# An encoder layer on one core: the gathers of neighbourhood values on ScalarE's queue, and own buffers for the sine products

## The chip, the cores and the metric

The kernel runs on one NeuronCore of a Trainium2 chip. A core has five engines that run at the same time, each through its own queue in order: TensorE (PE) multiplies matrices, VectorE (DVE) and ScalarE (ACT) work on elements, GpSimd (POOL) does small element work and issues DMAs, SyncE (SP) issues DMAs. Sixteen DMA engines move data between the device's DRAM (HBM) and the on-chip memory SBUF, or from DRAM to DRAM. PE writes its results into PSUM, eight banks of 128 x 512 float32.

The metric is device time in microseconds (us) for one execution, the median of several runs. The profile comes from one further execution.

## What is computed

One layer of a bidirectional encoder on 1024 tokens of width 1024, in float32: a half-step SwiGLU feed-forward block, a token mixing block, a second half-step feed-forward block, each with normalisations around it. Cut to the token mixing, where the change lies:

```python
def _rotary(x, pos):
    ...
    cos, sin = jnp.cos(ang), jnp.sin(ang)
    x1, x2 = x[..., :half], x[..., half:]
    return jnp.concatenate([x1 * cos - x2 * sin, x1 * sin + x2 * cos], axis=-1)

def _token_mixing(u, w_in, ...):
    rq, rk, rv, rg, nq, nk, nv, g_ret, g_na = jnp.split(u @ w_in, points, axis=-1)
    q = _rotary(heads(rq, RET_QK_DIM), pos)
    k = _rotary(heads(rk, RET_QK_DIM), pos) * (RET_QK_DIM ** -0.5)
    y = _bidirectional_retention(q, k, heads(rv, RET_V_DIM), ...)
    ...
    y_ret = (jax.nn.silu(rg) * y) @ w_ret_out
    y_na = _neighborhood_attention(na_heads(nq), na_heads(nk), na_heads(nv), rel_bias) @ w_na_out
    merged = jax.nn.sigmoid(g_ret) * y_ret + jax.nn.sigmoid(g_na) * y_na
    return merged @ w_out
```

The neighbourhood attention sees the tokens as a grid of 16 rows by 64 columns. A block of 16 query columns looks at a window of 32 key columns, so the values nv are needed in four overlapping sets of columns (32 columns starting at 0, 8, 24 and 32).

## The kernel before

**Arithmetic.** Every float32 operand of a matrix product is split into a high part, a copy cast on ACT (L62), and a low part, the difference, on DVE (L63). A product of two split operands is three matmuls (L94 to L96). Weights come in by SP as blocks of 128 x 1024 (`wraw`, four buffers, L73) and are split into pieces `wh` and `wl`, eight buffers each.

**Winograd pairs.** Most of the projection u @ W runs in `Pairs`: a job takes two weight blocks g and u (512 KB each) and forms seven products of 128 x 512 in place of eight, named by the left operand: a11, s2, a12, s3, s1, a22, s4, in this order on PE, 12 matmuls each. The weight side needs sums of blocks: t1 (L550 or L574), t2 (L551 or L575), t3 (L587), t4 (L593 or L603). The four results c11, c12, c21, c22 are built on DVE out of the PSUM banks: L572 copies the first product on ACT, then come L578, L583, L590, L598, L600, L605 and L608. L608 is the last of a job; its instruction is kept as `mx.end`. Within a job, once its own last pieces are split, `prepare(i + 1)` loads the next job's two blocks and forms and splits what its first products need; the low part of the last piece prepared is kept as `mx.ahead`.

**The stage of the change.** The loop at L1434 runs 14 jobs. Jobs 0 to 3 make the attention's queries and keys. After job 3 the second half of nv is projected (`vproj`, L1463) and stored by POOL to DRAM as d["nv"]; then, before the change, SP issues four copies, DRAM to DRAM, that gather nv into the four column sets d["nvg"] (L1466, 1 MB each). Jobs 4, 6, 8 and 10 are the rotary ones (one head of queries and keys each), 5, 7, 9 and 11 the silu gates, 12 and 13 two sigmoid gates. The attention stage, which reads nvg (L966), begins after job 13.

**A rotary result.** For each of a rotary job's four parts, `done` (L1441) first carries out the swaps that are pending, then calls `rotate`: DVE multiplies the part by the sine table into a buffer t (L1110) and by the cosine table in place (L1111); POOL stores the cosine product to rq or rk. The swap, carried out when the next part is done, adds the two halves of t crosswise to what was stored, by two accumulating DMAs on POOL (L1115, L1116). Before the change, the parts and the buffers t take turns in one set of six buffers of 128 x 512 (`half()`, tag "ev").

**What sets the order.** A planner orders each engine's queue ahead of the run, by its own model of time; data dependencies and the reuse of buffers become semaphores. `c.after(e, names)` (L76) adds an edge that bears on the order alone (class NoSync).

Of the kernel before, what the change touches and what calls it, by code (L numbers as in the profile page):

```python
# [11 lines left out]
F32 = mybir.dt.float32  # L12
# [7 lines left out]
P = 128  # L20
# [8 lines left out]
NHP = 4  # L29
# [6 lines left out]
KEY_OFF = (0, 8, 24, 32)  # L36
# [1070 lines left out]
def rotate(c, t, x, cos, sin, dst, behind):  # L1107

    tt = c.nc.vector.tensor_tensor
    c.after(tt(t, x, sin, ALU.mult).ins, behind)  # L1110
    tt(x, x, cos, ALU.mult)  # L1111
    c.store(dst, x)

    def swap():
        c.nc.gpsimd.dma_start(dst[0:64], t[64:128], accum_op=ALU.add)  # L1115
        c.nc.gpsimd.dma_start(dst[64:128], t[0:64], accum_op=ALU.add)  # L1116
    return swap
# [159 lines left out]
def trunk_layer(ctx: ExitStack, tc, x, xt, g1a, w1i, w1o, g1b, gma, wmt, wnv, wrv, logits, dtab, rope, bias,  # L1277
                wro, wno, wmo, gmb, g2a, w2i, w2o, g2b, out):
    nc = tc.nc
# [5 lines left out]
    c = Core(tc, const, wpool, psum, dram)  # L1285
# [3 lines left out]
    def dt(name, shape):  # L1289
        return dram.tile(shape, F32, name=name)  # L1290
# [3 lines left out]
    d = {  # L1294
        "a21": dt("a21", [P, 4, 512]),
        "nq": dt("nq", [NHP, P, S]), "nk": dt("nk", [NHP, P, S]), "nv": dt("nv", [16, 64, 512]), "nvg": dt("nvg", [4, 4, P, 512]),
        "no": dt("no", [NHP, P, S]), "rq": dt("rq", [RH, P, S]), "rk": dt("rk", [RH, P, S]),
        "rv": dt("rv", [TT, P, D]), "rg": dt("rg", [8, P, S]), "ry": dt("ry", [8, P, S]),
        "dec": dt("dec", [P, 536]), "far": dt("far", [3, 2, P, 512]), "far1": dt("far1", [3, 2, P, 512]), "far2": dt("far2", [3, 2, P, 512]), "sr": dt("sr", [8, P, S]), "sn": dt("sn", [8, P, S]), "z": dt("z", [8, P, S]), "m": dt("m", [8, 2, P, S]),
    }  # L1300
# [6 lines left out]
    def pool(stack, name, side="left"):  # L1307
        return stack.enter_context(tc.tile_pool(name=name, bufs=1, side=side, reuse_waits="tile"))
# [52 lines left out]
    def vproj(src, groups, done):  # L1361

        w = []
        for toks in groups:
            banks = {t: c.bank() for t in toks}
            for k in range(KT):
                if k == len(w):
                    w += ahead.pop(k // 2) if k // 2 in ahead else c.load_w(src[k // 2])
                    if k > 3 and qk:
                        c.after(c.fetch, qk)  # L1370
                        qk.clear()
                for t in toks:
                    tt = slice((t % 4) * P, (t % 4 + 1) * P)
                    c.mm3(banks[t], [q[:, k % 4, tt] for q in xh(t // 4, k // 4)], w[k], k == 0, k == KT - 1)
                    yield
            for t in toks:
                done(t, banks[t])
# [27 lines left out]
    mx = Pairs(c, wx, [(wmt[j[0]], wmt[j[1]]) for j in jobs], 3, joined=False)  # L1405
# [15 lines left out]
    with tc.tile_pool(name="pa", bufs=1, reuse_waits="tile") as pa:  # L1421
        evpool[:] = [pa]
        fill.drain()
        swaps = []

        def half():
            return pa.tile([P, 512], F32, tag="ev", name="ev", bufs=6)

        tabs = [[pa.tile([P, 512], F32, tag="tab", name="tab", bufs=4) for _ in range(2)] for _ in range(2)]
        for h in range(2):  # L1430
            for j in range(2):
                nc.sync.dma_start(tabs[h][j], rope[:, j, h * 512:(h + 1) * 512])

        for i, (_, _, f, g, fn) in enumerate(jobs):  # L1434
            parts = {}

            def part(j):
                parts[j] = half()
                return parts[j]

            def done(j):  # L1441
                h = j % 2
                dst = (f, g)[j // 2][:, h * 512:(h + 1) * 512]
                while swaps:
                    swaps.pop()()
                if fn == "rotary":
                    swaps.append(rotate(c, half(), parts[j], *tabs[h], dst, [] if j == 0 else [mx.ahead]))
                    return
                if fn is not None:
                    nc.scalar.activation(parts[j], parts[j], fn)  # L1450
                c.store(dst, parts[j])
            mx.run(i, part, done, i not in (NHP - 1, len(jobs) - 1))
            if i == 2:
                x1pool = pool(x1_stack, "x1b", "right")
                a21[:] = [x1pool.tile([P, 4, 512], F32R, name=f"a21{q}") for q in "hl"]
                for k in range(2):
                    raw = c.raw(d["a21"][:, 2 * k:2 * k + 2].rearrange("p k t -> p (k t)"))
                    c.split(*[q[:, 2 * k:2 * k + 2].rearrange("p k t -> p (k t)") for q in a21], raw)
            if i == NHP - 1:
                dec = pa.tile([P, 536], F32, name="dec")  # L1460
                Decays(dec).make(c, pa, logits, dtab)
                c.store(d["dec"], dec)
                for _ in vproj(wnv, ((4, 5, 6, 7),), done_nv):  # L1463
                    pass
                for cb in range(4):
                    nc.sync.dma_start(d["nvg"][cb].rearrange("t (r c) d -> (t r) c d", r=4),  # L1466
                                      d["nv"][:, KEY_OFF[cb]:KEY_OFF[cb] + 32, :])
    left.close()

    m_stack, o_stack = ExitStack(), ExitStack()  # L1470
# [55 lines left out]
    tabs = mix.tile([P, 536], F32, name="dec")  # L1526
# [181 lines left out]
```

## Time and profile before

| | |
|---|---|
| median of 3 runs | 2209.81 us (2209.61 to 2209.9) |
| the profiled execution | 2210.64 us |
| its span, first to last instruction | 2208.9 us |
| granted TensorE clock | 0.999 of full speed |
| share of ACT and POOL busy | 43% and 27% |
| data moved | 444.63 MB, mean 201 GB/s |

How to read the rows below. A row of the table by windows has the stretch and its length in us, then the busy time of PE, of PE's weight loads (PEld), of DVE, ACT and POOL with the number of instructions, then the granted clock, the mean busy share of the DMA engines, and GB/s. A row of the timeline has start and duration in us, engine, line of the code, operation, what is written and read by the program's names, shape and count; in brackets stands the engine's idle time just before and what ended it. A row of one line of the code has its count, the least, median and greatest duration in ns, and the first and last start in us. SPq is SP's queue, on which issuing a DMA takes time; "DMA to landing" is from issue until the data are there. One matmul of 512 columns shows 0.39 us, but the next starts 0.227 us later, since they overlap.

### The profile page before, as it was taken

How to read it: one execution, taken by the hardware profiler on the slowest of the kernel's cores; microseconds unless marked ns; L12 is line 12 of the kernel's file. 1: busy time of each engine (PE TensorE's matmuls, PEld its weight loads, DVE VectorE, ACT ScalarE, POOL GpSimd, SP SyncE). 2: the span in 40 equal slices, each digit the busy share in tenths (PEclk: the TensorE clock that was granted, in tenths of full speed). 3: DMA queues.
4: the chain of work that ended last, by engine and by line, in shares of the span. 5: the costliest groups of instructions: out<-in, count | busy, mean ns of one | idle time of the engine just before them, and what ended most of it. 6: DMA issues, size and time to landing. Idle time of an engine off the chain costs nothing.

```text
span 2208.9 us, 29722 instructions
## 1 busy us (share of the span) xinstructions
PE 2186.8 (99%) x10232; PEld 1824.4 (83%) x10232; DVE 1574.1 (71%) x2767; ACT 959.9 (43%) x1970; POOL 588.7 (27%) x766
## 2 busy tenths in 40 slices
PE   8999999999999999999999999999999999999998
PEld 7878888888888888888888888888888888888887
DVE  7898887655569757777766677643999787867444
ACT  7444434322345322367775565322544343433232
POOL 2122212169421122311001222101112121216942
PEclk9999999999999999999999999999999999999999
DMA  7354544597745555575543466785446343549865
GB/s 267 129 194 173 200 167 169 220 374 284 246 174 188 197 170 145 146 237 180 184 168 128 145 210 222 272 303 185 156 153 226 130 170 133 181 170 373 276 224 185
DMA packets 151206, 444.63 MB, mean 201 GB/s; under 512 B 19472, under 2 KB 46224, under 8 KB 148944
## 3 DMA queue, kind: packets, MB, share of 16 engines
q1 hardware_dynamic: 107584, 302.97, 40.7%
q0 software_dynamic: 43472, 139.77, 17.6%
q8 instruction: 81, 1.33, 0.2%
q14 instruction: 69, 0.57, 0.1%
HBM read 294.54 MB, written 152.32 MB: 202 GB/s over the span
## 4 chain that ended last, share of the span: by engine, by line
PE 90%; DVE 4%; issue 3%; ACT 1%; DMA 1%; POOL 1%; POOLq 0%; SPq 0%; DVEq 0%; ACTq 0%
PE ps L94 28%; PE ps L95 28%; PE ps L96 28%; PE pt L95 1%; PE pt L94 1%; PE pt L96 1%; PE pt L1002 1%; PE ps L983 1%; DMA g0s<-gth 1%; PE pt L133 0%; DVE wl L63 0%; PE pt L1216 0%; POOL rstd L104 0%; DMA gt<-in_dram 0%; POOL g0a L69 0%
## 5 line engine op out<-in xcount | busy, mean ns | idle before, releaser
L63 DVE TENSOR_TENSOR wl<-wraw,wh 128x512 fp32r<-128x512 f32 x440 | 292.4, 686 | 54.1 <-ACT wh L62 53.3
L62 ACT CAST wh<-wraw 128x512 fp32r<-128x512 f32 x444 | 255.2, 618 | 135.2 <-PE ps L95 57.4
L94 PE MATMUL ps<-wh,g 128*128 128x512 f32 x548 | 214.1, 391 | 0.4 <-DVE tmp L231 0.4
L95 PE MATMUL ps<-wl,g 128*128 128x512 f32 x548 | 213.6, 390 | 0.0
L96 PE MATMUL ps<-wh,g 128*128 128x512 f32 x548 | 213.3, 389 | 0.0
L63 DVE TENSOR_TENSOR wl<-w,wh 128x512 fp32r<-128x512 f32 x77 | 78.8, 1044 | 83.9 <-ACT wh L62 83.7
L63 DVE TENSOR_TENSOR wl<-x,wh 128x512 fp32r<-128x512 f32 x77 | 79.9, 1054 | 76.1 <-ACT wh L62 74.6
L62 ACT CAST wh<-t 128x512 fp32r<-128x512 f32 x58 | 36.1, 622 | 212.2 <-DVE t L575 130.4
L94 PEld LDWEIGHTS ps<-wh,g 128*128 128x128 f32 x548 | 102.9, 188 | 22.0 <-DVE tmp L231 0.7
L95 PEld LDWEIGHTS ps<-wl,g 128*128 128x128 f32 x548 | 102.9, 188 | 21.4 <-DVE wl L63 0.7
L96 PEld LDWEIGHTS ps<-wh,g 128*128 128x128 f32 x548 | 102.9, 188 | 21.3
L94 PE MATMUL ps<-a11h,wh 128*128 128x512 f32 x276 | 108.7, 395 | 1.5 <-ACT a11h L62 1.5
L94 PE MATMUL ps<-a22h,wh 128*128 128x512 f32 x280 | 109.7, 392 | 0.0
L95 PE MATMUL ps<-a11l,wh 128*128 128x512 f32 x276 | 107.9, 391 | 1.3 <-DVE a11l L63 1.3
L95 PE MATMUL ps<-a22l,wh 128*128 128x512 f32 x280 | 109.1, 390 | 0.0
L96 PE MATMUL ps<-a22h,wl 128*128 128x512 f32 x280 | 109.0, 389 | 0.0
L96 PE MATMUL ps<-a11h,wl 128*128 128x512 f32 x276 | 107.7, 390 | 0.9 <-DVE wl L63 0.9
L94 PE MATMUL ps<-a12h,wh 128*128 128x512 f32 x276 | 108.2, 393 | 0.0
L95 PE MATMUL ps<-a12l,wh 128*128 128x512 f32 x276 | 107.5, 390 | 0.0
L96 PE MATMUL ps<-a12h,wl 128*128 128x512 f32 x276 | 107.5, 389 | 0.0
L62 ACT CAST wh<-w 128x512 fp32r<-128x512 f32 x77 | 46.6, 620 | 110.8 <-PE pt L96 54.5
L69 POOL DMA_DIRECT2D g1a<-gth x33 | 17.9, 543 | 285.1 <-ACT gth L672 284.3
(444 smaller groups left out, 6305.5 us busy)
## 6 DMA issues: line engine op xcount, KB each, us to landing
wraw<-in_dram SPq DMA_DIRECT2D x190, 512.0 KB, 4.4
g<-g0s SPq DMA_DIRECT2D x44, 512.0 KB, 4.2
g<-g1s SPq DMA_DIRECT2D x44, 512.0 KB, 4.5
g<-g0a SPq DMA_DIRECT2D x33, 512.0 KB, 4.7
g<-g1a SPq DMA_DIRECT2D x33, 512.0 KB, 4.7
g0s<-gth POOLq DMA_DIRECT2D x44, 256.0 KB, 4.0
g0s<-cmb POOLq DMA_DIRECT2D x44, 256.0 KB, 3.9
g1s<-gth POOLq DMA_DIRECT2D x44, 256.0 KB, 3.9
```

What stands on the lines that cost most here:

```text
L62: self.done = [nc.scalar.copy(h, src).ins, (eng or nc.vector).tensor_tensor(l, src, hf, ALU.subtract).ins]
L63: (eng or nc.vector).tensor_tensor(l, src, hf, ALU.subtract).ins]
L69: self.nc.gpsimd.dma_start(dst, src)
L94: mm(ps, a[0], b[0], start=start, stop=False, skip_group_check=again)
L95: mm(ps, a[0], b[1], start=False, stop=False, skip_group_check=again)
L96: self.tail = mm(ps, a[1], b[0], start=False, stop=stop, skip_group_check=again).ins.name
L983: nc.tensor.matmul(bv, q[:, rg * P:(rg + 1) * P], k, start=n == 0, stop=n == 1)
L1002: nc.tensor.transpose(pt[:, j * P:(j + 1) * P], s[:, i % 2, (i // 2) * P:(i // 2 + 1) * P], c.ident)
```

## The change

The buffers t of the rotary jobs come from a set of four of their own (tag "evt"); the parts keep the six "ev" buffers to themselves. The four gathers of nv are written one job later in the program, after job 4 (`i == NHP`) in place of job 3, on ACT's queue in place of SP's, with an ordering edge behind the last DVE instruction of job 4 (`mx.end`).

```diff
                 if fn == "rotary":
-                    swaps.append(rotate(c, half(), parts[j], *tabs[h], dst, [] if j == 0 else [mx.ahead]))
+                    swaps.append(rotate(c, pa.tile([P, 512], F32, tag="evt", name="evt", bufs=4), parts[j], *tabs[h], dst, [] if j == 0 else [mx.ahead]))
                     return
...
                 for _ in vproj(wnv, ((4, 5, 6, 7),), done_nv):
                     pass
+            if i == NHP:
                 for cb in range(4):
-                    nc.sync.dma_start(d["nvg"][cb].rearrange("t (r c) d -> (t r) c d", r=4),
-                                      d["nv"][:, KEY_OFF[cb]:KEY_OFF[cb] + 32, :])
+                    c.after(nc.scalar.dma_start(d["nvg"][cb].rearrange("t (r c) d -> (t r) c d", r=4),
+                                                d["nv"][:, KEY_OFF[cb]:KEY_OFF[cb] + 32, :]).ins, [mx.end.name])
```

## The prediction

> **What bounds the kernel now.** I began with the page's busy times, then cut the span into stages with the table of busy time by windows, then asked what TensorE (PE) waited for.
>
> ```profile
> PE 2186.8 (99%) x10232; PEld 1824.4 (83%) x10232; DVE 1574.1 (71%) x2767; ACT 959.9 (43%) x1970; POOL 588.7 (27%) x766
> 0.00:100.00 100.00, 92.38 (x409) 75.61 (x410) 80.85 (x130) 58.07 (x109) 13.27 (x21) 1.00 0.51 184
> 100.00:780.00 680.00, 677.35 (x3012) 558.76 (x3011) 509.52 (x807) 267.45 (x502) 222.70 (x275) 1.00 0.60 215
> 780.00:840.00 60.00, 60.00 (x266) 49.68 (x265) 34.03 (x54) 17.40 (x30) 15.11 (x23) 1.00 0.66 197
> 840.00:860.00 20.00, 19.07 (x84) 15.27 (x83) 16.02 (x27) 5.08 (x9) 7.77 (x11) 1.00 0.41 82
> 860.00:960.00 100.00, 100.00 (x442) 82.82 (x442) 75.13 (x121) 37.91 (x64) 27.64 (x41) 1.00 0.60 162
> 960.00:1000.00 40.00, 39.32 (x198) 32.61 (x197) 27.05 (x69) 25.12 (x59) 6.13 (x8) 1.00 0.80 259
> 1000.00:1400.00 400.00, 398.19 (x2272) 347.46 (x2271) 283.61 (x734) 255.17 (x650) 72.00 (x109) 1.00 0.55 178
> 1400.00:1600.00 200.00, 199.20 (x909) 164.69 (x908) 118.72 (x192) 72.20 (x150) 23.25 (x40) 1.00 0.65 230
> ```
>
> PE is busy for 2186.8 of 2208.9 us, so all its idle time is 22.1 us, and 10.3 us of it lie before 780, where the change does not reach (7.6 in the first 100 us, 2.65 in the next 680). The change lies between about 787 us, where job 4 begins, and 940. There PE loses time in one stage only, 840 to 860. The rows of PE and of VectorE (DVE) at that place say why:
>
> ```profile
> 787.51 0.39 PE L94 MATMUL ps<-a11h,wh 128*128 128x512 f32 x1
> 806.55 0.39 PE L94 MATMUL ps<-a11h,wh 128*128 128x512 f32 x1
> 825.59 0.39 PE L94 MATMUL ps<-a11h,wh 128*128 128x512 f32 x1
> 844.63 0.39 PE L94 MATMUL ps<-a11h,wh 128*128 128x512 f32 x1
> 846.18 0.50 PE L96 MATMUL ps<-a11h,wl 128*128 128x512 f32 x1 [0.93 <-DVE wl L63]
> 865.05 0.39 PE L94 MATMUL ps<-a11h,wh 128*128 128x512 f32 x1
> 844.83 0.69 DVE L608 TENSOR_TENSOR ev<-ps,ev 128x512 f32<-128x512 f32 x1 [2.03 <-PE ps L96]
> 845.44 0.68 DVE L63 TENSOR_TENSOR wl<-wraw,wh 128x512 fp32r<-128x512 f32 x1
> 846.15 0.69 DVE L550 TENSOR_TENSOR wraw<-wraw 128x512 f32<-128x512 f32 x1
> ```
>
> The five a11h,wh rows are the first matmuls of jobs 4 to 8. Jobs 4, 5 and 6 take 19.04 us each (806.55 - 787.51, and so on): seven products of 2.72 us. Job 7 takes 865.05 - 844.63 = 20.42, so the stall and the matmuls just behind it cost **1.38 us**. PE waited for the low part (L63) of job 7's first weight piece, and on DVE that stood in the queue behind L608 of job 6, which needs job 6's last product. Job 7's whole preparation (L550 and what follows) came behind it too. So in this stage the wait that ends last is one of DVE's order, not of DVE's speed.
>
> **The change, part by part.** First, the gathers (L1466): four copies of 1 MB, DRAM to DRAM, leave SyncE's (SP's) queue for ScalarE's (ACT's), behind L608 of job 4.
>
> ```profile
> L1466 SPq DMA_DIRECT2D nvg<-nv x4: 557/718/1382, 793.3 to 796.2; - x4
> L1466 SPq EVENT_SEMAPHORE  x2: 28/3231/6434, 786.8 to 793.3; - x2
> DMA to landing us min/median/max: 7.0/10.4/13.1
> 793.33 3.51 SPq L1466 DMA_DIRECT2D nvg<-nv  x4
> 816.77 14.24 SPq L73 DMA_DIRECT2D wraw<-in_dram  x4
> 814.68 0.59 ACT L572 COPY ev<-ps 128x512 f32<-128x512 f32 x1 [11.79 <-PE ps L95]
> 816.05 1.90 DVE L63 TENSOR_TENSOR wl<-wraw,wh 128x512 fp32r<-128x512 f32 x3
> ```
>
> SP loses a wait of 6.43 us and 3.51 us of issue. Behind them stands the weight load (L73) at 816.77, which waits for the first of the three L63 at 816.05 (it ends at 816.7), 20 us after the gathers were issued. So SP's relief is worth **0** by itself. On ACT, no DMA is issued in this trace. The bounds are 0 and SP's longest, 4 x 1.382 = 5.5 us; I take SP's 3.51, the same four copies. The wait on the stores of nv is over by 793.3, before job 4's L608, so it costs nothing. The edge that is added (the helper at L76) only orders; it sets no semaphore. PE ends job 4 at 806.55, so ACT can issue from about 807.2 to 810.7, at the far bound to 812.7. Behind it stands job 5's copy L572, whose product is done at 806.55 + 2.72 = 809.3 and which ran at 814.68 before; PE wants that bank back only six products later, at 806.55 + 6 x 2.72 = 822.9. Cost **0**, from both bounds. If that cover were gone, the price would be the same 3.5 us.
>
> Second, the sine products (L1110) no longer take turns in the six ev buffers.
>
> ```profile
> 798.31 0.54 POOL L69 DMA_DIRECT2D rq<-ev  x1 [9.18 <-DVE ev L1111]
> 809.81 0.89 POOL L1115 DMA_DIRECT2D rq<-ev  x1 [10.96 <-DMA rq<-ev]
> 809.61 0.69 DVE L1110 TENSOR_TENSOR ev<-ev,tab 128x512 f32<-128x512 f32 x1 [3.97 <-DMA rq<-ev]
> 814.07 0.69 DVE L1110 TENSOR_TENSOR ev<-ev,tab 128x512 f32<-128x512 f32 x1 [1.36 <-DMA rq<-ev]
> 820.74 0.69 DVE L590 TENSOR_TENSOR ev<-ps,ev 128x512 f32<-128x512 f32 x1 [1.41 <-DMA rk<-ev]
> 793.30:805.60 12.30, 12.30 (x56) 10.20 (x55) 9.51 (x15) 2.19 (x4) 0.54 (x1) 1.00 0.99 347
> 826.19 1.14 POOL L1116 DMA_DIRECT2D rk<-ev  x1
> 834.67 0.69 DVE L1110 TENSOR_TENSOR ev<-ev,tab 128x512 f32<-128x512 f32 x1
> ```
>
> The first store of rq, issued at 798.31 while the gathers held the DMA engines (share 0.99 from 793.3 to 805.6), took about 11 us, and DVE stood still for a buffer: 3.97 + 1.36 + 1.41 = 6.74 us in three waits. All three should go: the store no longer meets the gathers, and the product has a buffer of its own. What that moves is the weight load, which waits for L63: two of the waits stand ahead of 816.05, so the load for job 6 can go out up to 5.33 us earlier, at about 811.4. PE did not wait in these 6.74 us (60.00 of 60.00 busy), so by itself this is also worth **0**. It pays only through job 6 and job 7: with DVE, loads and pieces of job 6 earlier, job 7's preparation can stand ahead of L608 as it does in every other job, and the 1.38 us go. Bounds: 0 and 1.38. The new buffers bring a wait of their own: four hold one rotary job's products, so job 6's first (834.67) waits until the last accumulation of job 4 (issued at 826.19) has read its buffer. 8.5 us lie between, and what would queue behind it on DVE is L1111 and L590, beside a busy PE: 0. Of the whole part I take 1.38: the two late things ahead of this place, gathers and buffer waits, are the very ones the change removes.
>
> Third, memory: four buffers of 512 x 4 bytes, 8 KB a partition, in the pool's top.
>
> ```profile
> 936.57 1.13 POOL L1116 DMA_DIRECT2D rk<-ev  x1
> L940 SPq DMA_DIRECT2D qraw<-nq x16: 450/589/605, 957.5 to 1084.7; - x16
> ```
>
> Their last reader is issued at 936.57; even at the gathers' 13.1 us it lands by 949.7. The attention stage, which reuses this memory, loads from 957.5. Cost 0.
>
> **Sum**: 0 + 0 - 1.38 + 0 = -1.4 us. The profiled execution took 2210.64 (span 2208.9), 0.83 above the median of the runs, 2209.81. So 2209.3 for a profiled execution, **2208.4** as median. About 0.2%, or 4.4 us, is what a measurement of this kernel can tell from no change. All idle time of PE from 780 to 1600 is 0.93 + 0.68 + 1.81 + 0.80 = 4.2 us, so there is not even room for a gain of that size in the stages that follow.
>
> **Rivals.** *It is hidden altogether.* DVE's order is fixed ahead of the run by a planner, and the profile does not say why it put job 7's preparation late. If it stays so, every saved wait lies beside a busy PE, and the time is 2209.8. For it: PE shows no idle time at either removed wait. Against: the two causes of lateness are gone. The Trainium skill, "DMA: Bandwidth & Descriptors", section "Issuing engines are not separate DMA queues", says that issuing from several engines saves only the issuer's time, small beside the transfer; by that rule the first part gives nothing, and the trace agrees (SP had nothing ready to issue before 816.77).
>
> *The gathers now collide with the weight loads, and the kernel is slower.* They were in flight from 793 to about 809; they move to about 807 to 823, and there lie the loads for job 6 and the rotary stores and accumulations:
>
> ```profile
> 816.80:822.00 5.20, 5.20 (x25) 4.30 (x24) 3.70 (x6) 2.17 (x3) 2.30 (x4) 1.00 1.00 208
> 821.35 0.68 DVE L550 TENSOR_TENSOR wraw<-wraw 128x512 f32<-128x512 f32 x1
> L62 ACT CAST wh<-wraw 128x512 fp32r<-128x512 f32 x444 | 255.2, 618 | 135.2 <-PE ps L95 57.4
> wraw<-in_dram SPq DMA_DIRECT2D x190, 512.0 KB, 4.4
> ```
>
> The DMA share there is already 1.00. Job 6's load landed in time for L550 at 821.35, and PE needs the piece's low part at 825.59 + 0.23 = 825.8; a cast (0.62) and L63 (0.69) lie between, so landing after 824.5 stalls PE. Issued at 816.77 and taking 13.1 us like the slowest gather, it would land at 829.9: a stall of 5.4 us, 2215.2. Issued at 811.4, the same 13.1 us land just at 824.5 and cost nothing. So it decides only where the load does not move ahead, or takes even longer. The Trainium skill, same page, section "Queues, rings and completion order", has each DMA engine take turns between the queues; by that rule a load on SP's queue would take about twice its usual 4.4 us beside ACT's (an estimate) and land by 820, with no stall. No run here has two such queues at once.
>
> *The planner's order shifts further on.* The stages from 960 to 1600 lose 0.68 + 1.81 + 0.80 = 3.3 us in short waits; another order could win part of them or add as much: 2206 to 2212.
>
> **Chances.** The stall goes and nothing else moves (2208.4, say 2207.9 to 2208.9): 0.47. Hidden (2209.8): 0.26. Collision (2210 to 2215.2): 0.15, of which 0.04 by over 4.4 us. Order elsewhere: 0.12, of which 0.02 beyond 4.4 us faster and 0.01 slower. So faster 0.02, within 0.2% 0.93, slower 0.05. The range reaches over the first two cases, the milder half of the collision and most of the last: 2207.0 to 2211.2.
>
> **What would show it.** Right: no wait of PE between 840 and 860, and job 7 taking 19.04 us; no wait of L1110 for a DMA of rq; the gathers' issues on ACT near 807, with L572 behind them not late for PE; job 6's load near 811. Wrong: PE waiting for a wl or wh at the start of job 6 near 825.6 (collision), job 7 still at 20.4 (hidden), or other waits after 960 (order).

## The result and the profile after

| | before | after |
|---|---|---|
| median | 2210.09 us (2208.85 to 2211.95, 22 runs) | 2213.07 us (2211.84 to 2215.88, 22 runs) |
| the profiled execution | 2210.64 | 2211.95 |
| its span | 2208.9 | 2210.2 |

After over before is 1.0014, with a 95% interval of 1.0008 to 1.002: about 3.0 us slower. That lies within the 0.2% forecast as "same", but above the range, and on the other side of the 1.4 us gain that was predicted.

First the table by windows of after; its columns are those of the prediction's table (length, PE, PEld, DVE, ACT, POOL, granted clock, DMA share, GB/s).

```profile
710.00:730.00 20.00, 16.20 (x69) 12.44 (x68) 14.38 (x47) 3.55 (x8) 2.16 (x4) 1.00 0.34 119
780.00:840.00 60.00, 60.00 (x267) 49.69 (x266) 34.71 (x55) 17.72 (x30) 14.05 (x21) 1.00 0.65 193
840.00:860.00 20.00, 20.00 (x90) 16.58 (x89) 15.80 (x26) 4.96 (x9) 6.93 (x9) 1.00 0.65 144
860.00:960.00 100.00, 100.00 (x443) 82.84 (x442) 74.83 (x121) 38.13 (x64) 29.45 (x43) 1.00 0.56 152
```

From 780 to 960 PE never stands still: the stall of 840 to 860 is gone, as forecast. But from 710 to 730, some 60 us ahead of every line that the diff touches, PE is busy for 16.20 of 20 us. The prediction had no row of that stage. Here is its row of the kernel before, with PE's wait there, the first DVE instruction of the retention's decays, and the two loads on SP that will matter:

```profile
710.00:730.00 20.00, 19.23 (x85) 15.58 (x85) 15.70 (x44) 4.37 (x10) 2.71 (x5) 1.00 0.32 112
716.65 0.50 PE L94 MATMUL ps<-s1h,wh 128*128 128x512 f32 x1 [0.78 <-DVE ev L586]
705.92 0.17 DVE L1074 TENSOR_SCALAR dect<-decx 128x8 f32<-128x8 f32 x1
692.76 2.24 SPq L1432 DMA_DIRECT2D tab<-in_dram  x4
695.04 0.47 SPq L1071 DMA_DIRECT2D decx<-in_dram  x1
```

And the timeline of after, PE, then DVE, then SP:

```profile
717.04 0.50 PE L94 MATMUL ps<-s1h,wh 128*128 128x512 f32 x1 [2.44 <-DVE ev L586]
720.24 0.50 PE L94 MATMUL ps<-a22h,wh 128*128 128x512 f32 x1 [0.18 <-DVE ev L590]
724.47 0.50 PE L94 MATMUL ps<-s4h,wh 128*128 128x512 f32 x1 [1.18 <-ACT ev L572]
705.27 0.69 DVE L583 TENSOR_TENSOR ev<-ps,ev 128x512 f32<-128x512 f32 x1 [0.26 <-ACT ev L572]
714.68 0.17 DVE L1074 TENSOR_SCALAR dect<-decx 128x8 f32<-128x8 f32 x1 [8.72 <-DMA decx<-in_dram]
716.30 0.69 DVE L586 TENSOR_TENSOR ev<-ps,ev 128x512 f32<-128x512 f32 x1
704.62 1.88 SPq L1432 DMA_DIRECT2D tab<-in_dram  x4
706.54 1.00 SPq L1071 DMA_DIRECT2D decx<-in_dram  x1
```

Read from the bottom. The load of `decx` (L1071), 128 x 8 numbers from which the decays of the retention are made, goes out at 706.54 where it went out at 695.04, and so do the rotary tables ahead of it (704.62 in place of 692.76). The decays' first DVE instruction that reads it (L1074) stands at the head of DVE's queue and waits 8.72 us for it; before, it ran at 705.92 without a wait. Behind it in that queue is L586 of job 0, the instruction that empties a PSUM bank that PE wants: PE stands for 2.44 us. Two waits of 0.18 and 1.18 us follow while DVE and ACT catch up; before, one wait of 0.78 was there.

The first matmuls of jobs 4, 7 and 8 make the account:

```profile
789.88 0.39 PE L94 MATMUL ps<-a11h,wh 128*128 128x512 f32 x1
847.00 0.39 PE L94 MATMUL ps<-a11h,wh 128*128 128x512 f32 x1
866.04 0.39 PE L94 MATMUL ps<-a11h,wh 128*128 128x512 f32 x1
```

Job 4 begins at 789.88 against 787.51 before, 2.37 us late. Job 7 takes 866.04 - 847.00 = 19.04 us against 20.42, so 1.38 are won back, and job 8 begins 0.99 late. The two spans differ by 1.3. The medians differ by 3.0; the profiled execution of after was one of its fastest (2211.95, where the lowest of 22 runs is 2211.84), and the runs of one kernel differ by up to 3.1 us before and 4.0 after, so a single pair need not show the difference of the medians. The last section comes back to the 1.7 us that this pair does not show.

### The profile page after: what moved, and what is told of

It reads as the page before. It is cut to its first block, busy times and chain, and to the rows that moved or that the text cites. A ratio compares the mean times of both kernels' runs of the same rounds, so it can differ in the third digit from the quotient of the medians.

```text
span 2210.2 us, 29703 instructions
## 1 busy us (share of the span) xinstructions
PE 2186.6 (99%) x10232; PEld 1824.4 (83%) x10232; DVE 1573.5 (71%) x2767; ACT 959.8 (43%) x1970; POOL 586.5 (27%) x766
## 4 chain that ended last, share of the span: by engine, by line
PE 86%; DVE 5%; issue 4%; ACT 2%; DMA 2%; POOL 1%; SPq 0%; POOLq 0%; DVEq 0%; ACTq 0%
PE ps L94 27%; PE ps L95 27%; PE ps L96 27%; PE pt L94 1%; PE pt L96 1%; PE pt L95 1%; DVE wl L63 1%; PE pt L1002 0%; ACT s L988 0%; PE ps L983 0%; POOL rstd L104 0%; DMA no<-ot 0%; DMA decx<-in_dram 0%; PE pt L133 0%; DVE s L984 0%
## 5 line engine op out<-in xcount | busy, mean ns | idle before, releaser
L63 DVE TENSOR_TENSOR wl<-wraw,wh 128x512 fp32r<-128x512 f32 x440 | 292.8, 688 | 56.7 <-ACT wh L62 56.1
L63 DVE TENSOR_TENSOR wl<-w,wh 128x512 fp32r<-128x512 f32 x77 | 78.9, 1045 | 83.7 <-ACT wh L62 83.6
L63 DVE TENSOR_TENSOR wl<-x,wh 128x512 fp32r<-128x512 f32 x77 | 79.9, 1055 | 77.2 <-ACT wh L62 75.8
```

Source lines behind the costliest of these rows:

```text
L63: (eng or nc.vector).tensor_tensor(l, src, hf, ALU.subtract).ins]
```

## The experiments

**The theory.** The pool `pa` holds the buffers "ev", the rotary tables, the decays' small tiles and now "evt". It begins before job 0. In the program's memory map it takes bytes 128864 to 152768 of a partition before the change, and reaches 160960 after. At 153440 begin the tiles `cmb`, in which the sums of the Winograd operands are formed until about 704 (L299 at 701.71 and L300 at 702.92 write the last). The longer pool lies over them, so the plan opens it, as a whole, later; the loads of its tables come about 12 us later, and `decx` is late at the head of DVE's queue. **The rivals:** that the loss comes of the use of the four buffers or of the gathers' new place; or that any edit reshuffles the order.

The first two rows below are SP's weight loads beside these loads, before and after; the third is DVE's last read of `cmb`, after.

```profile
704.82 1.53 SPq L73 DMA_DIRECT2D wraw<-in_dram  x2
703.04 1.53 SPq L73 DMA_DIRECT2D wraw<-in_dram  x2
704.30 0.69 DVE L63 TENSOR_TENSOR s4l<-cmb,s4h 128x512 fp32r<-128x512 f32 x1
```

They say how the lateness reaches the run. Two weight loads that stood behind the loads of the pool before (704.82) stand ahead of them after (703.04), and the tables go out right behind, at 704.62. The last read of `cmb` lasts until 704.99, so the first of these loads did not wait for that memory in the run; the later opening acts through the place in SP's queue that the plan gives to the loads.

A first group of four takes the change apart. The ratios are to the kernel before, whose median was 2210.01 us in these comparisons. In `gathers_only` the sine products of the changed kernel go back into the six shared buffers:

```diff
-                    swaps.append(rotate(c, pa.tile([P, 512], F32, tag="evt", name="evt", bufs=4), parts[j], *tabs[h], dst, [] if j == 0 else [mx.ahead]))
+                    swaps.append(rotate(c, half(), parts[j], *tabs[h], dst, [] if j == 0 else [mx.ahead]))
```

> The four gathers on ACT's queue behind job 4, as in the change, but the sine products back in the six ev buffers. Theory (the new buffers do the harm, by making pool pa longer than 153440 bytes from the start of SBUF, onto the sums of the Winograd operands): no trace of it here. DVE does not wait for decx, PE is busy about 19.2 of the 20 us from 710 to 730 as before the change, and the time is 0 to 1.4 us below before. Rival (the gathers' new place makes the planner order the tables and the decays another way): PE busy 16 to 17 us from 710 to 730, and 1.5 to 4 us above before.

In `buffers_only` the same two lines are exchanged the other way in the kernel before, and the gathers stay where they were:

```diff
-                    swaps.append(rotate(c, half(), parts[j], *tabs[h], dst, [] if j == 0 else [mx.ahead]))
+                    swaps.append(rotate(c, pa.tile([P, 512], F32, tag="evt", name="evt", bufs=4), parts[j], *tabs[h], dst, [] if j == 0 else [mx.ahead]))
```

> Four buffers of their own for the sine products, the gathers back on SP's queue behind job 3. Theory (the buffers do the harm): DVE waits about 8.7 us for decx near 706, PE is busy about 16.2 us from 710 to 730, and the time is 2 to 4.5 us above before. Rival (the gathers' new place does it): 710 to 730 as before the change, time within 1.4 us of before. From 840 to 860 PE is busy 20.0 us if the buffers alone cure the wait at the start of job 7, 19.1 if the gathers are needed for it.

In `own_pool` the four buffers of the changed kernel lie at the same addresses, but in a pool that is opened before job 4:

```diff
...
+            if i == NHP:
+                spare.append(pool(t_stack, "evt"))
...
-                    swaps.append(rotate(c, pa.tile([P, 512], F32, tag="evt", name="evt", bufs=4), parts[j], *tabs[h], dst, [] if j == 0 else [mx.ahead]))
+                    swaps.append(rotate(c, spare[0].tile([P, 512], F32, tag="evt", name="evt", bufs=4), parts[j], *tabs[h], dst, [] if j == 0 else [mx.ahead]))
```

> The whole change, but the four buffers lie in a pool of their own at the same addresses, opened after job 3. Theory (what hurts is that pool pa as a whole waits for the memory that its longest end needs): tables and decays come as before the change, PE is busy 19.2 us from 710 to 730 and 20.0 from 840 to 860, and the time is 0.5 to 1.5 us below before. Rival (four more buffers in that memory hurt wherever they are declared, or the gathers do it): 16 to 17 us busy from 710 to 730, time 1.5 to 4 us above before.

In `decays_later` the pool is as long as in the change, and the decays' first DVE instructions (in `Decays.make`, L1074 and on) are ordered behind L608 of job 0, which is what `behind` holds:

```diff
-        nc.vector.tensor_scalar(a, x, -1.0, None, ALU.mult)
+        for op in (nc.vector.memset(s, 1.0 / 17.0), nc.vector.tensor_scalar(a, x, -1.0, None, ALU.mult),
+                  nc.vector.tensor_scalar(lg, x, 0.0, None, ALU.min)):
+            c.after(op.ins, behind)
...
-        nc.vector.memset(s, 1.0 / 17.0)
...
-        nc.vector.tensor_scalar(lg, x, 0.0, None, ALU.min)
...
-                Decays(dec).make(c, pa, logits, dtab)
+                Decays(dec).make(c, pa, logits, dtab, [ends[0]])
```

> The whole change, with one ordering edge more: the first DVE instructions of the decays stand behind the last one of job 0. Theory (the price is DVE's wait for decx at the head of its queue, with L586 of job 0 behind it): the tables still come late, but DVE works on job 0 meanwhile; PE is busy at least 19 us from 710 to 730, and the time is 0.5 to 1.5 us below before. Rival (PE's loss comes of the late loads themselves, or of the weight loads that changed places with them): still 16 to 17 us from 710 to 730 and 1.5 to 4 us above before.

| kernel | median us | ratio, 95% interval | PE 710 to 730 | 780 to 840 | 840 to 860 |
|---|---|---|---|---|---|
| before | 2210.01 | 1 | 19.23 | 60.00 | 19.07 |
| gathers_only | 2215.46 | 1.0025 (1.0015 to 1.0035) | 19.25 | 56.19 | 20.00 |
| buffers_only | 2213.02 | 1.0015 (1.0006 to 1.0024) | 16.78 | 60.00 | 19.07 |
| own_pool | 2208.80 | 0.9995 (0.9986 to 1.0004) | 19.28 | 60.00 | 20.00 |
| decays_later | 2207.64 | 0.9989 (0.998 to 0.9997) | 20.00 | 60.00 | 20.00 |

The last three columns are PE's busy time in the three stretches by each kernel's windows. They say which part of the change makes which loss. The loss of 710 to 730 is there with the buffers in `pa`, and goes with either cure: a shorter `pa`, or the decays moved away from the head of DVE's queue. In `decays_later` the load of `decx` still goes out late, at 707.21, and PE loses nothing by it, so the late loads alone are not the price. The stall of job 7 (840 to 860) goes with the gathers' move alone and stays with the buffers alone. In time `decays_later` gained 2.4 us, more than the 0.5 to 1.5 that were expected; the two stalls that it removes, 0.78 and 1.38 us, make 2.2 of them.

`gathers_only` went against what was expected of it: it is the slowest of all, by a loss that neither parent kernel has. Its timeline, POOL, DVE, SP, PE, and then its windows:

```profile
805.12 0.60 POOL L69 DMA_DIRECT2D rk<-ev  x1 [3.32 <-DVE ev L1111]
819.00 0.87 POOL L1115 DMA_DIRECT2D rk<-ev  x1 [11.51 <-DMA rk<-ev]
815.18 0.69 DVE L1110 TENSOR_TENSOR ev<-ev,tab 128x512 f32<-128x512 f32 x1 [7.35 <-DMA rq<-ev]
825.68 0.69 DVE L590 TENSOR_TENSOR ev<-ps,ev 128x512 f32<-128x512 f32 x1 [4.58 <-DMA rk<-ev]
826.29 1.28 DVE L63 TENSOR_TENSOR wl<-wraw,wh 128x512 fp32r<-128x512 f32 x2
820.53 6.79 SPq L73 DMA_DIRECT2D wraw<-in_dram  x2
827.03 0.79 PE L96 MATMUL ps<-s4h,wl 128*128 128x512 f32 x1 [3.47 <-DVE wl L63]
823.50:827.00 3.50, 0.06 (x1) 0.00 (x0) 1.31 (x3) 0.00 (x0) 0.00 (x0) 0.89 0.86 236
827.00:830.00 3.00, 2.97 (x7) 2.39 (x8) 2.97 (x5) 0.63 (x1) 1.26 (x3) 0.50 0.60 186
830.00:833.00 3.00, 3.00 (x8) 2.32 (x8) 3.00 (x6) 2.70 (x5) 2.13 (x4) 0.50 0.92 191
```

The gathers go out at 801.1 to 802.9 and take up to 15.2 us. The store of `rk` at 805.12 lies beside them and takes over 11 us; the accumulation behind it on POOL waits 11.51 us for it, and the shared buffers are held as long. DVE waits 7.35 and 4.58 us for a buffer. The second of these waits is L590's; right behind it stands the L63 (826.29) that PE wants in job 5's last product, and PE stops for 3.47 us. SP's load for job 6 (820.53) is late too, behind another L63, but PE does not wait for it. Then the granted clock is 0.50 for about 6 us, which costs some 3 us more (an estimate: 6 us at half the clock). In `own_pool` the same gathers meet the same store, and POOL waits as long, but DVE does not wait for a DMA, and the loads for job 6 are on their way 8 us earlier:

```profile
818.80 0.87 POOL L1115 DMA_DIRECT2D rk<-evt  x1 [11.60 <-DMA rk<-ev]
812.46 17.81 SPq L73 DMA_DIRECT2D wraw<-in_dram  x4
```

So the buffers have a use: they make the gathers' place behind job 4 harmless.

The second group goes for the length of the pool by itself. Both pads add one tile to the kernel before, which nothing reads or writes; the first leaves the pool 160 bytes short of `cmb`, the second, with 512 in place of 128, reaches over it.

```diff
+            if i == NHP:
+                pa.tile([P, 128], F32, name="evt")
```

> The kernel before, with one more tile of 512 bytes a partition in the pool pa, which nothing reads or writes. The pool then ends 160 bytes short of the tiles cmb, in which the sums of the Winograd operands lie. Theory (the pool waits for the memory under its far end): nothing changes, the decays' table is loaded near 695 us, PE is busy for 19.2 of the 20 us from 710 to 730, and the time is that of the kernel before, ratio 0.999 to 1.001. Rival (any change of the pool's contents reshuffles the order, or the time of the new buffers is one of their use and not of their place): this rival says nothing else for this kernel; it is told apart by the run with the 2048 bytes.

> The kernel before, with one more tile of 2048 bytes a partition in the pool pa, which nothing reads or writes; the pool now reaches over the first bytes of the tiles cmb. Theory: the whole pool is opened only when cmb is free, the load of the decays' table goes out near 706 us in place of 695, DVE stands 8 to 9 us at the head of its queue for it, PE is busy for 16 to 17 of the 20 us from 710 to 730, and the median is 2 to 4.5 us above the kernel before, as with the four buffers in use. Rival (the loss comes of the use of the four buffers, their waits and their order, not of the pool's length): 19.2 of 20 and the time of the kernel before.

| kernel | median us | ratio, 95% interval | PE 710 to 730 | 840 to 860 |
|---|---|---|---|---|
| before | 2210.16 | 1 | 19.23 | 19.07 |
| pad_512 | 2210.23 | 0.9999 (0.999 to 1.0007) | 19.27 | 19.07 |
| pad_2048 | 2214.30 | 1.0018 (1.0009 to 1.0027) | 16.15 | 19.07 |

DVE and SP of `pad_512`:

```profile
706.22 0.19 DVE L1074 TENSOR_SCALAR dect<-decx 128x8 f32<-128x8 f32 x1
695.11 0.49 SPq L1071 DMA_DIRECT2D decx<-in_dram  x1
```

and of `pad_2048`:

```profile
714.81 0.18 DVE L1074 TENSOR_SCALAR dect<-decx 128x8 f32<-128x8 f32 x1 [8.77 <-DMA decx<-in_dram]
706.64 0.95 SPq L1071 DMA_DIRECT2D decx<-in_dram  x1
```

A tile that no instruction touches makes the loss as the change made it: the load 11.5 us later, a wait of 8.77 us (after: 8.72), 16.15 us of PE (after: 16.20). The same tile at a quarter of the size does nothing. That the loss comes of the pool's far end is shown; that the border lies at 153440 is the memory map's word, the runs place it between the two sizes.

The same group asks what the cures are worth apart and together: `before_decays` is the kernel before with the edit of `decays_later`, `own_decays` is `own_pool` with it.

> The kernel before, with nothing of the change, but with the first DVE instructions of the decays ordered behind the last DVE instruction of job 0. Theory (the two gains are separate: the decays' place is worth the 0.8 us for which PE waited on L586, the change's first part the 0.9 us and more at job 7): PE is busy for 20.00 of 20 us from 710 to 730 and still 19.07 from 840 to 860; the median is 0.5 to 1.5 us below the kernel before, and above that of the changed kernel with the decays so ordered (2207.6). Rival (the order behind moves as well, and job 7's stall goes by the decays alone): 20.00 in both stretches and a median within 0.5 us of 2207.6.

> The changed kernel, with the four buffers in a pool of their own that is opened before job 4, and with the first DVE instructions of the decays ordered behind the last DVE instruction of job 0. Theory (the pool's length hurts only through the decays' table at the head of DVE's queue): both cures mend the same loss, so that together they give what the ordering alone gives, PE 20.00 of 20 from 710 to 730 and from 840 to 860, median 2206.8 to 2208.2. Rival (the late opening costs elsewhere too, in the 12 us by which the loads and the first copies come later): 0.5 to 1.5 us better than the ordering alone, 2206 to 2207.

`before_decays`: 2209.72 us, ratio 0.9997 (0.9988 to 1.0006), PE 20.00 from 710 to 730 and 19.07 from 840 to 860. `own_decays`: 2208.05 us, 0.9989 (0.9981 to 0.9998), 20.00 and 20.00. The traces are the theory's: the ordering takes away the 0.78 us of L586, and leaves job 7 as it was. In time the first gave 0.4 us of the 0.5 to 1.5 expected, with an interval on both sides of 1. The two cures together give what the ordering alone gave, so the late opening costs nothing else that these runs can tell.

The last pair asks whether the gathers could do without the buffers. Both start from `gathers_only`, with the six shared buffers, and put the gathers behind job 5, when no rotary job has just ended; `job5_decays` has the ordering of the decays as well.

```diff
-            if i == NHP:
+            if i == NHP + 1:
```

> The changed kernel with the parts and the sine products sharing the six buffers again, and the gathers on ACT's queue one job later still, behind job 5 in place of job 4. Theory (the loss of the run with the gathers alone, 3.8 us of PE between 780 and 840, comes of the gathers lying beside job 4's rotary stores, which then hold the shared buffers for 11 us; nothing is stored to rq or rk while job 6 multiplies): PE 60.00 of 60 from 780 to 840, no stall of 3 us and no drop of the granted clock near 827; from 840 to 860 20.00 of 20, since the gathers are off SP's queue here too; 19.2 of 20 from 710 to 730. Median 2208 to 2210. Rival (the shared buffers lose time with the gathers on ACT's queue wherever these lie): a loss of 2 us or more between 820 and 900, median 2212 or more.

> The same, with the first DVE instructions of the decays also ordered behind the last DVE instruction of job 0. Theory (the new buffers are needed only to make the gathers harmless behind job 4; behind job 5 the six buffers do): PE 20.00 of 20 from 710 to 730 and from 840 to 860, 60.00 of 60 between, median 2207 to 2208.3, as the changed kernel with the same ordering (2207.6), without the 8 KB. Rival (the new buffers win something of their own, the DVE waits behind the stores): 0.5 to 1.5 us slower than that, 2208.2 to 2209.2.

`gathers_job5`: 2208.85 us against 2210.29, ratio 0.9993 (0.9984 to 1.0002). `job5_decays`: 2208.52, 0.9993 (0.9984 to 1.0002). From 780 to 860 PE is busy for all 80 us in both; from 710 to 730 it is 19.23 and 20.00. The gathers go out at 824.3 to 826.5, and PE waits for nothing that comes of it. The store of `rk` that took over 11 us in `gathers_only` is done so soon here that POOL waits 0.48 us for it: what hurt there was the gathers' place beside job 4's stores. Some waits are left beside a busy PE: DVE stands 1.5 us for a store of `rq` (848.21), POOL 6.12 us (843.78). `job5_decays` came 0.2 us above its expected range and within that of its rival (2208.2 to 2209.2); whether the buffers win something of their own, these runs can't tell.

Of all these, `decays_later` and `own_decays` alone have intervals wholly below 1, against the kernel before: by about 2.4 and 2.1 us. `decays_later` also beats the changed kernel: its interval ends at 0.9997 of the kernel before, and the changed kernel's begins at 1.0008.

## Why the prediction was wrong

**The step that failed** is "Third, memory: four buffers of 512 x 4 bytes, 8 KB a partition, in the pool's top. ... Cost 0." It asked who uses this memory after the buffers, and that answer holds (960 to 1000 has 39.32 us of PE before and after). It did not ask who uses it ahead of them. The term was +3.0 us by `buffers_only` (2213.02 - 2210.01), not 0. The profile of before held the row that could have warned: the wait of 0.78 us for L586 just behind the decays, of which the prediction saw only a sum, "2.65 in the next 680", and called it a stretch "where the change does not reach".

**The gain at job 7** was right in size, 1.38 us, and in place. Its cause was put wrong: the prediction credited "gathers and buffer waits" together and booked the gain under the buffers. `buffers_only` keeps the stall and `gathers_only` loses it, so it is the gathers' move alone. Why the planner then put job 7's preparation ahead of L608 no trace says; that it did is in DVE's rows of the changed kernel, where job 7's L550 stands 8 us ahead of job 6's L608:

```profile
839.65 0.68 DVE L550 TENSOR_TENSOR wraw<-wraw 128x512 f32<-128x512 f32 x1
847.82 0.69 DVE L608 TENSOR_TENSOR ev<-ps,ev 128x512 f32<-128x512 f32 x1
```

**"The store no longer meets the gathers"** was half true. The first store of rq no longer does: the accumulation behind it waits 2.05 us in the changed kernel, not 10.96. The store of rk meets them now: 10.94 us in the changed kernel (11.51 in `gathers_only`, 11.60 in `own_pool`). With the gathers there, the three DVE waits went only since the products had buffers of their own; in `gathers_only` waits of 7.35 and 4.58 us stand in their place.

**The gathers on ACT** cost nothing, as forecast. The edge did not hold them behind L608, though the prediction took it to: they were issued ahead of it.

```profile
L1467 ACTq DMA_DIRECT2D nvg<-nv x4: 548/608/611, 804.0 to 805.8; - x4
809.74 0.69 DVE L608 TENSOR_TENSOR ev<-ps,ev 128x512 f32<-128x512 f32 x1
811.90 0.59 ACT L572 COPY ev<-ps 128x512 f32<-128x512 f32 x1 [6.64 <-PE ps L96]
```

It orders the plan alone, and in the run ACT came to them before DVE came to L608. Behind them L572 waited only for PE.

**The rivals.** The collision was real, though not with this change whole: without the buffers it cost 5.4 us (2215.46 - 2210.01). That is by chance the price that the rival named; the way was another. The prediction let job 6's load be slow and PE stand at the start of job 6; in the run PE stood in job 5's last product, because a held buffer stopped DVE, and about half of the price was the clock. None of the rivals was what happened: the measured 2213.07 lies in the band given to the collision, but in the changed kernel PE waits for nothing at job 6. "The planner's order shifts further on" had the right kind of cause and looked in the wrong direction: the order shifted 60 us ahead of the edit, not behind 960.

**The sum, mended,** is 0 - 1.4 + 3.0 = +1.6 us. Measured were +3.0, with an interval of 1.8 to 4.4 (1.0008 and 1.002 of 2210); the pool's term itself is known to 1.3 to 5.3 (1.0006 to 1.0024). So the two agree within what was measured, and no better.

## What to carry to other kernels

When a change adds a tile to a pool, ask of the memory under its new end not only who needs it next but who still holds it when the pool is opened: here 8 KB that no instruction touched before 799 us cost 3 us near 715, through a load that came 12 us later. A short chain that nothing needs soon, such as the decays, belongs behind the work that PE waits for: at the head of DVE's queue its one late load held up all that followed for 8.72 us, and an ordering edge mended it. And test the parts of a two-part change apart: alone, each of these lost time (3.0 and 5.4 us), for different reasons.

## What the runs showed of the hardware

A stall of PE can cost more than its length. In `gathers_only` PE stood for 3.47 us and the granted clock was 0.50 in the next 6 us. After 2.94 us in `buffers_only` it was 0.65 and 0.67 in two windows of 2.5 us:

```profile
718.64 0.79 PE L94 MATMUL ps<-s1h,wh 128*128 128x512 f32 x1 [2.94 <-DVE ev L586]
717.50:720.00 2.50, 1.36 (x3) 1.16 (x4) 2.19 (x12) 0.00 (x0) 0.00 (x0) 0.65 0.00 0
720.00:722.50 2.50, 2.50 (x9) 1.94 (x8) 2.33 (x10) 0.00 (x0) 0.00 (x0) 0.67 0.00 0
```

After 2.44 us in the changed kernel it stayed at 1.00, as it did in `pad_2048` after a wait of 2.5. A busy PE at half its clock is still busy, so the column of busy time does not show this; the column of the clock does. The Trainium skill, "TensorE: Matmul & The Clock Gate", section "Part 1: The HAM clock gate", has the clock fall to half after an idle window of about 3.4 us, by windows that run freely and so may or may not take in a given stall. The row of 3.47 us agrees; the fall after 2.94 came below its figure, and there the measurement decides. If the stall of 710 to 730 brings the clock down in some executions and not in others, it would cost those up to 2.5 x 0.35 + 2.5 x 0.33 = 1.7 us more, by the rows of `buffers_only`. That would be as much as lies between the medians' difference, 3.0, and that of the two profiled executions, 1.3. The windows of the clock are known for one execution of each kernel only, but a mean granted clock is on record for every run. Over the 22 runs of the changed kernel it averages 0.9980, over 31 of the kernel before 0.9987; 0.0007 of 2210 us is 1.5 us. That points the same way. Yet the six runs of the changed kernel with the lowest clock, 0.997, took 2212.9 us on average and the five with 0.999 took 2213.3, so within one kernel the clock and the time do not go together, and this stays open.
